# Norm weight, bias and alpha of the residual, moved from GpSimd to VectorE and from the norm to the next products

## The chip, the cores and the metric

One core of one Trainium2 chip. The metric is the device time of one execution in microseconds, as the median over runs. All data starts and ends in the chip's memory; float32 in and out.

## What is computed

Two layers of a diffusion block on 512 tokens of x and 256 of a context, 1024 channels wide. Each layer has a feed-forward (2816 wide, gated), four mixers side by side (windowed attention, a state space model, full attention, neighbourhood attention) with a common output product, and a second feed-forward. After each of the three branches comes a norm, post_norm; the norm's result is what the next branch reads, and times ALPHA it is also what the next branch's result is added to.

```python
ALPHA = (2 * DEPTH) ** 0.25          # DEPTH = 2

def post_norm(x, f, g, b):
    return layer_norm(ALPHA * x + f, g, b)

for l in range(DEPTH):
    x = post_norm(x, 0.5 * m[:, 2] * swiglu(modulate(x, m[:, 0], m[:, 1]), ffn1_w_in[l], ffn1_w_out[l]), ln_g[l, 0], ln_b[l, 0])
    ...
    x = post_norm(x, m[:, 5] * mix_x, ln_g[l, 1], ln_b[l, 1])
    x = post_norm(x, 0.5 * m[:, 8] * swiglu(modulate(x, m[:, 6], m[:, 7]), ffn2_w_in[l], ffn2_w_out[l]), ln_g[l, 2], ln_b[l, 2])
```

The context goes through the same steps with its own modulations m; in the last layer only its first feed-forward and norm are needed.

## The kernel before, in words

**Tiles.** The residual lies in SBUF as six tiles res of 128 tokens by 1024 channels: XT are the four of x, CT the two of the context. Products run on TensorE in float32r, each operand split in two parts whose sum it is, so a product is three matmuls (mm3, L329 to L331). Weights come by DMA on SP's queue into wraw or wrax; ScalarE rounds them into the first part wh (L322), VectorE subtracts for the second part wl (L323). Six slots of wh and wl let the splits run ahead of the products.

**Stages in time.** First feed-forward of layer 0 to about 600 us, mixers to 1046, the merge (the mixers' output product) to 1110, second feed-forward to 1705; in layer 1 the feed-forward to 2255, mixers to 2620, merge to 2665, the last feed-forward to the end.

**A branch's end.** Each accumulated product of 512 columns is multiplied by its modulation (add, L468) and added to the residual (L470) on VectorE. stats (L411 to L436) takes mean and variance, finds the reciprocal root for two tiles at a time by a chain of 13 small VectorE instructions (rsqrt, L394 to L400, then L432), and ScalarE normalises the tiles in place (L436). Then turn transposes a normalised tile on TensorE (L383); ScalarE scales and shifts it by channel, with the norm's weight and bias folded in, into S (L385); the cast L387 and VectorE's subtraction L388 make the two parts acth and actl, the left operands of the next products. The four x tiles are turned first, the context's two later.

**The residual's addend.** The tile itself still holds the normalised values, without weight and bias. rescale makes of them what the next branch's result is added to: ALPHA * (g * x + b). Its gain (L447) loads weight and bias onto all partitions by two DMAs, ScalarE multiplies both by ALPHA (L456), and for each tile and each half of its columns GpSimd multiplies and adds in place (L461): four instructions of 128x512 for a tile, 112 in all. They must wait until TensorE has transposed the tile. rescale is a generator with one step for each tile. The x tiles' steps are taken at once after the norm (branch_out, ffn); the context's follow one for each chunk of the next feed-forward (winograd), or at the spill.

**The feed-forward.** Its 22 chunks of 128 columns of gate and up weights: the first two as plain products, the rest by Winograd's seven products, for which GpSimd makes sums of weight tiles (L605, L606, L611, L613) and VectorE sums of products (L688 to L702). The result is split into gTh and gTl (L642, L643). The chunks come in parts; after the chunks of a part (lo .. hi) their part of the second product is added to the residual.

**Mixers.** Their scratch takes the room of the residual, so spill_res copies it to DRAM (away, L362) and fetch_res brings it back (L366) before the merge.

**Order.** A scheduler of the tile framework sets each engine's order of instructions from the order in which the code records them and from hints (issue_after: not ahead of that instruction).

Of the kernel before, what the change touches and what calls it, by code (L numbers as in the profile page):

```python
# [20 lines left out]
D = 1024  # L21
# [5 lines left out]
CT = (4, 5)  # L27
# [7 lines left out]
# columns of mix_w_in after the host's reordering (heads of aq and cq as 0, 2, 1, 3)  # L35
C_A, C_Z, C_XBC, C_C, C_D, C_BDT = 0, 512, 768, 1536, 2048, 2816

# columns of the constants
# [4 lines left out]
BY_SUM = (0, 4, 1, 5, 2, 6, 3, 7)  # channel chunks in the order of the feed-forward's sums  # L43
K_ID, K_SEL = K_N, K_N + P
GATES = (2, 5, 8)  # the modulations that multiply a branch
N_SLOTS = 2 * len(GATES)
K_ALL = K_SEL + 4 * N_SLOTS
# columns of the neighbourhood masks
# [4 lines left out]
def _constants():  # L53
# [19 lines left out]
    # sums of the four groups' rows of the modulations; for those that multiply a branch, half of it  # L73
    # where it is a feed-forward's, with the bias in rows 16 and on
# [17 lines left out]
def bcast(ap, n):  # L92
    """Repeats the elements of a [p, a, ...] operand n times along a new last dimension."""
    s = list(ap.shape)
    return ap.unsqueeze(len(s)).to_broadcast(s + [n])


def bcast1(ap, n):
    """Repeats a [p, ...] operand n times along a new first free dimension."""
    s = list(ap.shape)  # L100
    return ap.unsqueeze(1).to_broadcast([s[0], n] + s[1:])
# [12 lines left out]
def side_by_side(a, na, b, nb):  # L114
    """Runs two generators, of na and nb steps, so that both last as long."""
    i = j = 0
    while i < na or j < nb:
        if j >= nb or (i < na and i * nb <= j * na):
            next(a, None)
            i += 1  # L120
        else:
            next(b, None)
            j += 1
    for g in (a, b):
        for _ in g:
            raise AssertionError("more steps than told")


class Block:
    def __init__(self, ctx, tc, t, out):  # L130
# [7 lines left out]
        # the products' left operands, by channel, in two parts: inputs of the feed-forward and of  # L138
        # the mixers, then what the mixers give
# [25 lines left out]
    # ---------------------------------------------------------------- small parameters  # L165
    def turned(self, rows, tag):
        """Vectors cut in rows of 128, turned so that the channel is the partition."""
# [16 lines left out]
    def conditioning(self):  # L184
        """silu(c) and silu(c_ctx) as stationary operands: any two of 32 columns, the others zero."""
# [13 lines left out]
        # modulations by channel: layer, which of the nine, chunk, stream  # L199
# [39 lines left out]
    def ada_batch(self, l, ns, pool, at_once=()):  # L239
        """Two steps for each of these 512 columns of both streams' modulations; the last also places them: by  # L240
        channel (a shift and a scale's, in order), or, of what multiplies a branch, as rows in DRAM."""
# [48 lines left out]
    def mod_affine(self, l, i, halves=((0, KD),), into=None):  # L290
        """Scale and shift, by channel, of what follows norm i of layer l (i = -1: the input)."""
# [15 lines left out]
    # ---------------------------------------------------------------- weights and products  # L307
    def weights(self, src, shape):
        """Loads float32 weights, contraction chunks by columns, and splits each chunk into two float32r parts
        whose sum it is."""  # L310
# [6 lines left out]
    def split_slot(self, raw, slot=None):  # L317
        """The two parts of chunks [p, chunk, columns], in up to 512 columns."""
# [7 lines left out]
    def mm3(self, out, a, b, start, stop):  # L326
        """out += a'b with a and b given in two parts."""
# [8 lines left out]
    # ---------------------------------------------------------------- residual stream  # L336
# [14 lines left out]
    def scale_input(self):  # L351
# [4 lines left out]
    def spill_res(self, n):  # L356
        """The residual's addend waits in DRAM while the mixers run."""
        for _ in self.behind:
            pass
# [8 lines left out]
    def new_sums(self, pool, tiles):  # L368
        """Room for what the feed-forward's sums come from: act's value, by channel chunk."""
# [3 lines left out]
    def turn(self, tiles, aff, ks=range(KD)):  # L373
        """xT of these token tiles: turned, scaled and shifted by channel, split."""
# [15 lines left out]
    def rsqrt(self, tmp, x, n, mul=1.0):  # L390
        """(x * mul + EPS) ** -0.5 of n columns: a guess from the exponent, three Newton steps."""
# [11 lines left out]
    def stats(self, t, dh, tmp, gain=None):  # L403
        """Mean and variance of the token tile's half; after a pair's last, the pair normalised in place; with
        gain, each tile by itself, and the result of it put out."""
# [37 lines left out]
    def gain(self, l, i, tmp, tags):  # L443
        """A norm's gain and bias, on all partitions."""
# [5 lines left out]
    def rescale(self, l, i, tiles, tmp):  # L450
        """Normalised tiles times the gain and plus the bias, times alpha: the next residual's addend. One step
        for each tile."""
        nc = self.nc
        gb = self.gain(l, i, self.side or tmp, ("mrow0", "mrow1"))
        for x in gb:
            nc.scalar.mul(x, x, ALPHA)  # L456
        for t in tiles:
            for lo, hi in ((0, 512), (512, D)):
                for x, op in zip(gb, (ALU.mult, ALU.add)):
                    r = self.res[t][:, lo:hi]  # L460
                    nc.gpsimd.tensor_tensor(r, r, x[:, lo:hi], op=op)  # L461
            yield

    def add(self, t, dh, acc, mrow, tmp, norm, gain=None):
        """512 columns of a product, times its modulation, to the residual."""
# [8 lines left out]
    def branch_out(self, l, i, tiles, steps, a_of, w_of, mrow, tmp, todo=None):  # L474
        """Adds a product, times its modulation, to the residual, 512 columns at a time; with todo, what
        comes of normalised tiles by number, the normalisation and that.

        steps: weight tiles' contraction chunks, in order; w_of(step, dh) loads one; a_of(k, t) the left
        operand's parts."""
# [29 lines left out]
        if norm:  # L509
            self.behind = self.rescale(l, i, tiles, tmp)  # L510
            for _ in XT if len(tiles) == 6 else XT[:3]:
                next(self.behind)

    def follow(self, todo, upto, end):
        """After products of which end is the last: what follows token tiles up to this one."""
# [4 lines left out]
    def turns(self, aff, tmp, tiles):  # L520
        """What to do when a token tile is normalised."""
# [5 lines left out]
    def mod_rows(self, l, which, pool, streams):  # L527
        """The modulation that multiplies a branch, on all partitions."""
# [7 lines left out]
    # ---------------------------------------------------------------- feed-forward  # L536
    # The first product, of all tokens A and a chunk's gate and up weights B: with tokens and channels
    # halved, A21 the second tokens' first channels, and B12 the up weights' first channels, Winograd's seven
    # products:
    #   S1 = A21 + A22, S3 = A11 - A21, S2 = A22 - S3, S4 = A12 - S2  # L540
    #   T1 = B12 - B11, T3 = B22 - B12, T2 = T3 + B11, T4 = B21 - T2
    #   U = A11 B11 + S2 T2, C11 = A11 B11 + A12 B21, C12 = U + S4 B22 + S1 T1,
    #   C21 = U + S3 T3 + A22 T4, C22 = U + S3 T3 + S1 T1
    # The first chunks have the plain eight, while the sums come.
    def left(self, name):
        """Four channel chunks of half of the tokens, in two parts."""
# [6 lines left out]
    def sums(self, pool):  # L553
        """S2, S3 and S4, then S1 in A21's place: two steps of two channel chunks each, then one."""
# [32 lines left out]
    def ffn_weights(self, l, w_in, f, pool):  # L587
        """B11, B21, B22 and T1 .. T4 in two parts."""
# [24 lines left out]
        last = tt(y[:, 1], y[:, 1], x[:, 0], op=ALU.subtract)  # L613
        put("T1", y[:, 1])
        return w, last

    def ffn(self, l, w_in, w_out, which, i, with_ctx, pool, after, parts, extra=None, final=False, early=()):
        """extra: work for the gaps, by feed-forward chunk. after: called when the next modulation is due,
# [85 lines left out]
        for lo, hi in parts:  # L704
# [10 lines left out]
            if lo == 0:  # L715
                for _ in self.behind:
                    pass
# [830 lines left out]
```

## Time and profile before

| | |
|---|---|
| median of 3 runs | 3099.47 us (3094.49 to 3105.36) |
| profiled execution, span | 3101.0 us, 44820 instructions |
| TensorE (PE) busy | 2913.0 us, 94% |
| VectorE (DVE) busy | 2216.5 us, 71% |
| ScalarE (ACT) busy | 1172.8 us, 38% |
| GpSimd (POOL) busy | 734.8 us, 24%, of which L461 171.8 us |

The runs were timed without the profiler; the profile is of one more execution, for which the span alone is known, from its first to its last instruction. It lies inside the interval of the runs.

### The profile page before, as it was taken

What the parts mean: (1) busy time and instruction counts of PE and PEld (TensorE: products, weight loads), DVE (VectorE), ACT (ScalarE), POOL (GpSimd) and SP (SyncE); (2) the same over time, 40 slices, a digit from 0 to 9 for tenths busy, and PEclk for the clock granted to TensorE, in tenths of its full rate; (3) what the DMA queues carried; (4) which work ended last, traced back from release to release, by engine and by line L of the source; (5) the groups of instructions that cost most, each with busy time, mean ns of one, the idle gap of its engine ahead of it and who ended that gap; (6) DMA issues with size and microseconds to landing.
All of it is one profiled execution on the core that took longest, in us unless ns stands there. A gap on an engine that the chain in (4) does not pass through costs nothing.

```text
span 3101.0 us, 44820 instructions
## 1 busy us (share of the span) xinstructions
PE 2913.0 (94%) x16772; PEld 2485.0 (80%) x16772; DVE 2216.5 (71%) x4258; ACT 1172.8 (38%) x2153; POOL 734.8 (24%) x532
## 2 busy tenths in 40 slices
PE   8999999999999989999999799999989989889996
PEld 5888888778787767888888689998967777778886
DVE  5666667875757587666577976668786666888779
ACT  4333223342256443322233433332343356434333
POOL 1222212220112034221121531222150120234323
PEclk9999999999999999999999899999989999999998
DMA  6443334131133213544443122221222232233231
GB/s 207 156 143 125 111 105 136 60 106 41 42 85 61 89 55 89 177 133 132 129 156 118 60 68 68 68 82 49 68 93 67 70 80 64 75 115 88 82 96 69
DMA packets 319533, 296.17 MB, mean 96 GB/s; under 512 B 16631, under 2 KB 245071, under 8 KB 319059
## 3 DMA queue, kind: packets, MB, share of 16 engines
q1 hardware_dynamic: 318259, 290.80, 30.5%
q0 software_dynamic: 1056, 2.49, 0.4%
q8 instruction: 133, 2.18, 0.3%
q14 instruction: 85, 0.70, 0.1%
HBM read 270.52 MB, written 7.39 MB: 90 GB/s over the span
## 4 chain that ended last, share of the span: by engine, by line
PE 57%; DVE 17%; issue 3%; ACT 2%; DMA 1%; POOL 0%; DVEq 0%; SPq 0%; ACTq 0%; POOLq 0%
PE ps L329 8%; PE ps L331 8%; PE ps L330 8%; PE psp L329 7%; PE psp L330 7%; PE psp L331 7%; DVE wl L323 4%; PE ps L1025 2%; PE ps L1066 2%; PE psp L1082 2%; DVE actl L388 2%; DVE tmp L468 1%; PE ps L260 1%; DVE res L470 1%; ACT wh L322 1%
## 5 line engine op out<-in xcount | busy, mean ns | idle before, releaser
L323 DVE TENSOR_TENSOR wl<-wraw,wh 128x512 fp32r<-128x512 f32 x600 | 465.0, 782 | 341.7 <-ACT wh L322 336.2
L322 ACT CAST wh<-wraw 128x512 fp32r<-128x512 f32 x600 | 369.6, 620 | 897.3 <-PE ps L331 470.7
L329 PE MATMUL psp<-acth,wh 128*128 128x384 f32 (+2 forms) x1592 | 532.6, 335 | 24.1 <-DVE e L700 19.0
L330 PE MATMUL psp<-actl,wh 128*128 128x384 f32 (+2 forms) x1592 | 526.1, 331 | 2.7 <-DVE actl L388 2.7
L331 PE MATMUL psp<-acth,wl 128*128 128x384 f32 (+2 forms) x1592 | 524.6, 330 | 0.7 <-DVE wl L323 0.7
L329 PEld LDWEIGHTS psp<-acth,wh 128*128 128x128 f32 x1592 | 303.7, 191 | 72.9 <-ACT wh L322 49.0
L329 PE MATMUL ps<-S,wh 128*128 128x384 f32 (+1 forms) x960 | 315.2, 328 | 17.9 <-DVE ffg L638 7.7
L330 PEld LDWEIGHTS psp<-actl,wh 128*128 128x128 f32 x1592 | 303.5, 191 | 16.3 <-DVE actl L388 3.6
L331 PEld LDWEIGHTS psp<-acth,wl 128*128 128x128 f32 x1592 | 303.8, 191 | 12.8 <-issue 1.9
L331 PE MATMUL ps<-S,wl 128*128 128x384 f32 (+1 forms) x960 | 312.0, 325 | 1.2 <-DVE wl L323 1.2
L330 PE MATMUL ps<-S,wh 128*128 128x384 f32 (+1 forms) x960 | 312.0, 325 | 0.0
L461 POOL TENSOR_TENSOR res<-res,mrow 128x512 f32<-128x512 f32 x112 | 171.8, 1565 | 461.6 <-PE ps L383 340.8
L322 ACT CAST wh<-wrax 128x512 fp32r<-128x512 f32 x280 | 173.4, 620 | 271.6 <-PE ps L330 160.8
L323 DVE TENSOR_TENSOR wl<-wrax,wh 128x512 fp32r<-128x512 f32 x280 | 255.2, 918 | 7.2 <-ACT wh L322 6.2
L329 PE MATMUL ps<-wh,gTh 128*128 128x512 f32 x594 | 234.6, 395 | 8.3 <-DVE tmp L468 8.3
L331 PE MATMUL ps<-wh,gTl 128*128 128x512 f32 x594 | 233.4, 393 | 0.0
L330 PE MATMUL ps<-wl,gTh 128*128 128x512 f32 x594 | 233.1, 392 | 0.0
L330 PE MATMUL ps<-actl,wh 128*128 128x384 f32 (+2 forms) x568 | 202.5, 357 | 24.3 <-DVE actl L388 24.2
L329 PEld LDWEIGHTS ps<-S,wh 128*128 128x128 f32 x960 | 183.5, 191 | 42.8 <-ACT wh L322 26.7
L331 PE MATMUL ps<-acth,wl 128*128 128x384 f32 (+2 forms) x568 | 200.3, 353 | 8.1 <-DVE wl L323 8.1
L329 PE MATMUL ps<-acth,wh 128*128 128x384 f32 (+2 forms) x568 | 202.6, 358 | 3.7 <-ACT wh L322 2.3
L470 DVE TENSOR_TENSOR res<-res,tmp 128x512 f32<-128x512 f32 x268 | 190.9, 744 | 0.6
(369 smaller groups left out, 5727.4 us busy)
## 6 DMA issues: line engine op xcount, KB each, us to landing
araw<-in_ada_w_dram SPq DMA_DIRECT2D x128, 512.0 KB
wraw<-in_ffn_w_out_dram SPq DMA_DIRECT2D x88, 512.0 KB
wraw<-in_ffn_w_in_dram SPq DMA_DIRECT2D x160, 256.0 KB
wrax<-in_ffn_w_in_dram SPq DMA_DIRECT2D x160, 256.0 KB
wraw<-in_mix_w_in_dram SPq DMA_DIRECT2D x44, 512.0 KB
wraw<-in_ffn_w_in_dram SPq DMA_DIRECT2D x16, 512.0 KB
wraw<-in_mix_w_out_dram SPq DMA_DIRECT2D x16, 512.0 KB
mrow<-mrow SPq DMA_DIRECT2D x10, 512.0 KB
```

Source lines behind the costliest of these rows:

```text
L260: nc.tensor.matmul(ps[32 * g:32 * g + 32, :], lhsT=self.cs[:, k, c0:c0 + 32], rhs=w[:, k - kk, :], start=i == 0 and k < 4, stop=i == len(n ...
L322: self.nc.scalar.copy(h, raw)
L323: self.nc.vector.tensor_tensor(lo, raw, h.bitcast(F32), op=ALU.subtract)
L329: mm(out, lhsT=a[0], rhs=b[0], start=start, stop=False)
L330: mm(out, lhsT=a[0], rhs=b[1], start=False, stop=False)
L331: return mm(out, lhsT=a[1], rhs=b[0], start=False, stop=stop)
L388: nc.vector.tensor_tensor(l, y, h.bitcast(F32), op=ALU.subtract)
L461: nc.gpsimd.tensor_tensor(r, r, x[:, lo:hi], op=op)
L470: nc.vector.tensor_tensor(r, r, y, op=ALU.add)
L1025: nc.tensor.matmul(ps[:, at:at + hi - lo], lhsT=q, rhs=part[:, lo:hi], start=i == 0, stop=i == 1)
L1066: nc.tensor.transpose(pt[:, j * P:(j + 1) * P], p[:, a:a + P], self.ident)
L1082: nc.tensor.matmul(out[64 * a:64 * a + 64, :], lhsT=v[:, kt, vcol:vcol + 64], rhs=pT[:, i], start=i == 0, stop=i == len(order) - 1)
```

## The change

rescale runs its tensor_tensor instructions on VectorE and by halves: the first 512 columns of all tiles, then the second. Nothing of it is done at the norm any more: self.behind holds the call itself, and it is made where the next products come to be added. In a feed-forward that is after the chunks of the first part, in the merge at its start (after the residual is fetched, so that what is spilled is now the normalised tile). At the merge it takes only the tiles that the merge needs. winograd no longer takes a step of it, spill_res no longer drains it. scale_input (the scaling of the kernel's input, on VectorE before and after) takes two arguments that it does not use, to be called in the same way. A side pool for gains is closed one chunk later (ada 4 for 3). The comments, which are removed too, are left out here.

```diff
-    def rescale(self, l, i, tiles, tmp):
+    def rescale(self, l, i, tmp, tiles=XT + CT, tags=("mrow0", "mrow1")):
         nc = self.nc
-        gb = self.gain(l, i, self.side or tmp, ("mrow0", "mrow1"))
+        gb = self.gain(l, i, self.side or tmp, tags)
         for x in gb:
             nc.scalar.mul(x, x, ALPHA)
-        for t in tiles:
-            for lo, hi in ((0, 512), (512, D)):
+        for lo, hi in ((0, 512), (512, D)):
+            for t in tiles:
                 for x, op in zip(gb, (ALU.mult, ALU.add)):
                     r = self.res[t][:, lo:hi]
-                    nc.gpsimd.tensor_tensor(r, r, x[:, lo:hi], op=op)
+                    nc.vector.tensor_tensor(r, r, x[:, lo:hi], op=op)
             yield
...
     def spill_res(self, n):
-        for _ in self.behind:
-            pass
...
         if norm:
-            self.behind = self.rescale(l, i, tiles, tmp)
-            for _ in XT if len(tiles) == 6 else XT[:3]:
-                next(self.behind)
+            self.behind = partial(self.rescale, l, i)
...
         def winograd(f, g, rest):
-            w, last = self.ffn_weights(l, w_in, f, pool)
-            if with_ctx or f > 3:  # of fewer tokens, after the sums
-                with self.tc.issue_after(last.ins):
-                    next(self.behind, None)
+            w = self.ffn_weights(l, w_in, f, pool)
...
             if lo == 0:
-                for _ in self.behind:
+                for _ in self.behind(pool, tiles):
                     pass
...
             if not final:
-                self.behind = self.rescale(l, i, tiles, pool)
-                for _ in XT:
-                    next(self.behind)
+                self.behind = partial(self.rescale, l, i)
...
     def merge(self, l, last, tmp):
         tiles = XT if last else XT + CT
+        for _ in self.behind(tmp, tiles, ("mrow1", "mrow2") if last else ("mrow0", "mrow1")):
+            pass
...
-        ada = {3: [aside]}
+        ada = {4: [aside]}
```

The lines of the changed kernel have other numbers: its L459 is L461 of before, L466 and L468 are L468 and L470, L392 to L398 are the root's L394 to L400, L430 is L432, L385 and L386 are L387 and L388, L360 is L362.

In the order of the instructions, VectorE before the first addition of layer 0's merge, as it was (res are the residual's tiles, wl second parts of weights, actl those of the merge's left operand):

```order
L1137 SCALAR_TENSOR_TENSOR actl_65<-ps_1983_9866,smT_378,acth_64 128x256
L323 TENSOR_TENSOR wl_10061<-wraw_10054,wh_10060 128x512
L323 TENSOR_TENSOR wl_10137<-wraw_10134,wh_10136 128x512
L323 TENSOR_TENSOR wl_10141<-wraw_10134,wh_10140 128x512
L323 TENSOR_TENSOR wl_10183<-wraw_10180,wh_10182 128x512
L323 TENSOR_TENSOR wl_10187<-wraw_10180,wh_10186 128x512
L323 TENSOR_TENSOR wl_10193<-wraw_10190,wh_10192 128x512
L468 TENSOR_TENSOR tmp_10100<-psp_9912,mrow_1993_9894 128x512
```

And as it is in the changed kernel; of the 24 L459 the last ones are shown, the 21 others stand right ahead of them, behind wl_10061:

```order
L459 TENSOR_TENSOR res_1986_9849<-res_1986_9849,mrow_1992_9865 128x512
L459 TENSOR_TENSOR res_1987_9850<-res_1987_9850,mrow_1992_9865 128x512
L459 TENSOR_TENSOR res_1988_9851<-res_1988_9851,mrow_1991_9864 128x512
L323 TENSOR_TENSOR wl_10137<-wraw_10134,wh_10136 128x512
L459 TENSOR_TENSOR res_1988_9851<-res_1988_9851,mrow_1992_9865 128x512
L323 TENSOR_TENSOR wl_10141<-wraw_10134,wh_10140 128x512
L323 TENSOR_TENSOR wl_10183<-wraw_10180,wh_10182 128x512
L323 TENSOR_TENSOR wl_10187<-wraw_10180,wh_10186 128x512
L466 TENSOR_TENSOR tmp_10100<-psp_9912,mrow_1993_9894 128x512
```

The weight differences that followed one another now stand behind the block of L459, and wl_10193 behind the first additions.

The second place is VectorE after the merge of layer 0, at the context's reciprocal root (rs), before:

```order
L398 TENSOR_TENSOR rs_2092_10455<-rs_2091_10454 128x2
L399 SCALAR_TENSOR_TENSOR rs_2092_10455<-rs_2092_10455,rs_2090_10453 128x2
L400 SCALAR_TENSOR_TENSOR rs_2091_10454<-rs_2092_10455,rs_2091_10454 128x2
L432 SCALAR_TENSOR_TENSOR bnm_10468<-bnmv_10364,rs_2091_10454 128x2
L387 CAST acth_64<-S_1997_9904 128x256
```

The same place in the changed kernel, the last round of the root and what follows it:

```order
L396 TENSOR_TENSOR rs_2092_10455<-rs_2091_10454 128x2
L459 TENSOR_TENSOR res_1985_9848<-res_1985_9848,mrow_2203_11133 128x512
L397 SCALAR_TENSOR_TENSOR rs_2092_10455<-rs_2092_10455,rs_2090_10453 128x2
L459 TENSOR_TENSOR res_1986_9849<-res_1986_9849,mrow_2203_11133 128x512
L398 SCALAR_TENSOR_TENSOR rs_2091_10454<-rs_2092_10455,rs_2091_10454 128x2
L459 TENSOR_TENSOR res_1983_9846<-res_1983_9846,mrow_2202_11132 128x512
L430 SCALAR_TENSOR_TENSOR bnm_10468<-bnmv_10364,rs_2091_10454 128x2
L459 TENSOR_TENSOR res_1984_9847<-res_1984_9847,mrow_2202_11132 128x512
L634 TENSOR_TENSOR ffg_10628<-ps_2104_10522,ffg_10628 128x512
```

One L459 stands between every two steps of the root; behind its last step more of them stand ahead of the context's first cast. The remaining ones stand among the first Winograd chunks.

The third place is SP's queue at the start of layer 0's mixers (wraw here the mixers' weight tiles), before:

```order
L313 DMA wraw_5501<-in_mix_w_in_dram 128x8x128
L447 DMA mrow_987_5363<-in_ln_g_dram 128x1024
L313 DMA wraw_5571<-in_mix_w_in_dram 128x8x128
L313 DMA wraw_5644<-in_mix_w_in_dram 128x8x128
L447 DMA mrow_988_5364<-in_ln_b_dram 128x1024
L313 DMA wraw_5715<-in_mix_w_in_dram 128x8x128
L362 DMA away_5393<-res_4_78 128x1024
L362 DMA away_5393<-res_5_79 128x1024
```

In the changed kernel:

```order
L313 DMA wraw_5400<-in_mix_w_in_dram 128x8x128
L313 DMA wraw_5471<-in_mix_w_in_dram 128x8x128
L360 DMA away_5363<-res_4_78 128x1024
L360 DMA away_5363<-res_5_79 128x1024
L360 DMA away_5363<-res_6_80 128x1024
L360 DMA away_5363<-res_7_81 128x1024
L313 DMA wraw_5541<-in_mix_w_in_dram 128x8x128
```

The x tiles' spills moved from behind the fifth weight tile to behind the second, and the loads of the norm's weight and bias left this place.

## Rows read from the trace of the kernel before

**Rows 1.** The page: busy shares, chain by engine.

```profile
PE 2913.0 (94%) x16772; PEld 2485.0 (80%) x16772; DVE 2216.5 (71%) x4258; ACT 1172.8 (38%) x2153; POOL 734.8 (24%) x532
...
PE 57%; DVE 17%; issue 3%; ACT 2%; DMA 1%; POOL 0%; DVEq 0%; SPq 0%; ACTq 0%; POOLq 0%
```

**Rows 2.** The line L461: count, ns (min/median/max), first and last start.

```profile
L461 POOL TENSOR_TENSOR res<-res,mrow x112: 1253/1646/1892, 599.9 to 2747.8; 128x512 f32<-128x512 f32 x112
```

**Rows 3.** Busy time by stretch: us, PE, PEld, DVE, ACT, POOL, PEclk, DMA, GB/s.

```profile
599.90:627.70 27.80, 18.19 (x61) 12.21 (x59) 27.41 (x30) 7.99 (x13) 23.88 (x16) 0.82 0.35 120
1111.90:1138.70 26.80, 15.06 (x59) 10.35 (x57) 26.44 (x29) 6.89 (x13) 25.35 (x16) 0.85 0.18 58
1706.90:1733.50 26.60, 13.89 (x60) 8.87 (x58) 26.36 (x26) 6.97 (x12) 25.37 (x16) 0.89 0.20 61
2255.80:2283.60 27.80, 18.01 (x61) 12.21 (x59) 27.42 (x30) 8.00 (x13) 23.49 (x16) 0.82 0.34 120
2672.00:2684.20 12.20, 6.38 (x35) 5.55 (x33) 11.96 (x15) 1.86 (x5) 11.68 (x8) 0.86 0.29 86
```

**Rows 4.** Chain of the stretch 1109 to 1140 us: start, duration, what.

```profile
1110.83 0.33 DVE acth L387
1111.17 0.60 DVE res L470
1111.77 0.60 DVE actl L388
1112.37 1.43 DVE acth L387
...
1133.70 1.15 DVE rs L398
...
1137.32 0.17 DVE rs L398
```

**Rows 5.** VectorE's groups by form, 1111.9 to 1138.7 us: count, busy us, mean ns.

```profile
L388 DVE TENSOR_TENSOR actl<-S,acth 128x512 fp32r<-128x512 f32 x8 | 12.7, 1611 | 0.0
...
L323 DVE TENSOR_TENSOR wl<-wraw,wh 128x512 fp32r<-128x512 f32 x3 | 2.0, 679 | 0.0
```

**Rows 6.** TensorE's waits, 599.5 to 650 us: total us, times, longest.

```profile
PE ps L330 <- DVE actl L388: 8.7, 6, 2.2
```

**Rows 7.** TensorE's waits, 1111 to 1160 us.

```profile
PE ps L383 <- ACT res L436: 5.9, 1, 5.9
PE ps L331 <- DVE wl L323: 5.3, 1, 5.3
```

**Rows 8.** Busy time by stretch, behind the first of rows 3.

```profile
627.70:650.00 22.30, 18.81 (x113) 16.39 (x114) 15.89 (x23) 12.87 (x24) 11.94 (x8) 0.92 0.18 64
```

**Rows 9.** VectorE's groups by form over the run.

```profile
L323 DVE TENSOR_TENSOR wl<-wrax,wh 128x512 fp32r<-128x512 f32 x280 | 255.2, 918 | 7.2 <-ACT wh L322 6.2
L470 DVE TENSOR_TENSOR res<-res,tmp 128x512 f32<-128x512 f32 x268 | 190.9, 744 | 0.6
```

**Rows 10.** Busy time by stretch, ahead of the merges' first additions.

```profile
1046.00:1074.00 28.00, 27.78 (x128) 22.82 (x129) 9.37 (x19) 7.83 (x12) 0.00 (x0) 1.00 0.57 216
2628.00:2643.00 15.00, 15.00 (x67) 12.41 (x67) 5.52 (x9) 4.35 (x7) 0.00 (x0) 1.00 0.54 175
```

**Rows 11.** VectorE's groups by form over the run: the context's casts.

```profile
L387 DVE CAST acth<-S 128x256 fp32r<-128x256 f32 x28 | 12.8, 461 | 18.4 <-ACT S L385 18.3
```

**Rows 12.** Busy time by stretch, first Winograd chunks.

```profile
1170.00:1200.00 30.00, 24.28 (x129) 23.04 (x128) 28.75 (x34) 12.69 (x24) 19.37 (x13) 0.94 0.43 130
2700.00:2770.00 70.00, 59.62 (x437) 57.60 (x438) 64.22 (x103) 32.87 (x68) 30.17 (x21) 0.92 0.37 113
```

**Rows 13.** VectorE's groups by form, 1172.9 to 1196 us.

```profile
L323 DVE TENSOR_TENSOR wl<-wrax,wh 128x512 fp32r<-128x512 f32 x7 | 10.1, 1456 | 0.0
L323 DVE TENSOR_TENSOR wl<-wraw,wh 128x512 fp32r<-128x512 f32 x3 | 4.2, 1397 | 0.0
```

**Rows 14.** GpSimd's groups by form, 2693 to 2750 us.

```profile
L606 POOL TENSOR_TENSOR wraw<-wraw 128x512 f32<-128x512 f32 x2 | 2.8, 1408 | 9.8 <-DVE wl L323 9.8
```

More of the change, by code (lines that the diff above doesn't have):

```diff
@@ L349, in load_streams, with scale_input @@
             self.nc.sync.dma_start(self.res[i], src)
-    def scale_input(self):
+    def scale_input(self, pool, tiles):
         for r in self.res:
@@ L612, in ffn_weights @@
         put("T4", y[:, 0])
-        last = tt(y[:, 1], y[:, 1], x[:, 0], op=ALU.subtract)
+        tt(y[:, 1], y[:, 1], x[:, 0], op=ALU.subtract)
         put("T1", y[:, 1])
-        return w, last
+        return w
     def ffn(self, l, w_in, w_out, which, i, with_ctx, pool, after, parts, extra=None, final=False, early=()):
@@ L1461, in layers @@
         b.constants()
-        b.behind = b.scale_input()
+        b.behind = b.scale_input
         ada = {}
```

## The prediction

> **What bounds the kernel now.** Start with the page's busy shares and chain. TensorE is busy for 94% of the span and carries 57% of the chain that ended last; VectorE carries 17% of it, GpSimd nothing [rows 1]. By shares alone, moving 112 GpSimd instructions of about 1.6 us [rows 2] to VectorE only loads an engine that matters. But a share is a mean, so the next view is the stretches. In the five stretches in which GpSimd runs its first L461 instructions after a norm (the fifth is shorter, 12 us), VectorE is busy for the whole stretch while TensorE is busy for 14 to 18 of 27 us, at a granted clock of 0.82 to 0.89 [rows 3]. In these 121.2 us TensorE is busy for 18.19 + 15.06 + 13.89 + 18.01 + 6.38 = 71.5 us and idle for 49.7.
>
> Why is VectorE so slow there? In the chain after the merge of layer 0 the same instruction changes its duration the moment L461 begins (1111.9 us): the cast L387 takes 0.33 us at 1110.83 and 1.43 at 1112.37, the subtraction L388 takes 0.60 at 1111.77, the two-column steps of the reciprocal root take 1.15 us and, once L461 is over at 1137.3, 0.17 [rows 4]. The mean of L388 in the stretch is 1611 ns; weight differences between the root's steps keep their 679 [rows 5]. So what GpSimd does off the chain is paid on the chain: two thirds of VectorE's time in these stretches is contention. TensorE waits there for VectorE's two parts (8.7 us, L388) or for the normalised context tile (5.9 us, L436) and a weight difference (5.3 us, L323) [rows 6, 7].
>
> **What the change removes.** All 112 instructions leave GpSimd; 104 come to VectorE, because layer 1's first norm now scales only the four x tiles at the merge (8 fewer). The two ScalarE multiplications per norm and the DMAs of gain and bias only change place.
>
> One stretch priced again without contention, the second of rows 3 (29 instructions, 26.44 us): eight L388 at 0.60, three L387 at 0.33, three weight differences and one L411 at 0.6, thirteen steps of the root's chain at 0.17 + 0.02 between them: 4.8 + 1.0 + 2.4 + 2.5 = 10.7 us. It saves 15.7 us of chain. The first stretch has 30 such instructions and comes to 11.5: 15.9 saved; the third is taken as the second, the fourth as the first. The fifth (15 instructions, eleven of the root and four splits) comes to about 4.2 us: 7.8 saved.
>
> How much of a chain saving reaches the end? TensorE's own work in the stretch must still be done, so a floor is its idle time there, and the idle of the 22 us behind it, where the second GpSimd run falls (22.3 - 18.8 = 3.5 in the first case) [rows 8]. For the norms ahead of the mixers: idle 9.6 + 3.5 = 13.1, chain 15.9, and some waiting for casts remains, because 0.60 + 0.33/2 per channel chunk is still no faster than TensorE's products of it. I take **12 each, 24** (9 to 16).
>
> **What it adds, place by place.** A VectorE instruction of the moved form (two SBUF inputs, 128x512) is there already: L470 at 744 ns mean [rows 9], 0.60 us to the next one in the chain [rows 4]. So 104 x 0.60 = 62 us come to VectorE; what counts is where.
>
> *Merge of layer 0* (24 instructions, nearly all in one piece ahead of the first addition). From 1046 to 1074 VectorE is busy 7.83 of 28 us, TensorE 27.78 [rows 10]. 24 x 0.60 = 14.4 us fit in the 20 idle ones; a weight difference behind the burst comes late, but the splits run several chunks ahead. Cost 0; if the cover fails, two of the 0.69 us differences and the 4 us between them, 4.
>
> *Merge of layer 1* (16, 9.6 us). From 2628 to 2643 VectorE has 15 - 4.35 = 10.6 us idle [rows 10], so it just fits, but two weight differences that stood ahead of the first addition now stand behind it. I take 2 (0 to 5).
>
> *The norms ahead of the second feed-forward of layer 0 and the first of layer 1.* Eight of 15 or 16 stand between the steps of the context's root, whose last step releases ScalarE and then TensorE: 8 x 0.60 = 4.8 us on the chain. The other seven or eight stand ahead of the first cast of the context, which before waited 18.3 us in four norms for ScalarE, 4.6 each [rows 11]: 4.2 to 4.8 us, covered. So 15.7 - 4.8 = **11 each, 22**. TensorE's idle there, 11.7 and 12.7 us, agrees. The remaining eight or nine go into the first two Winograd chunks. VectorE is busy for 28.75 of 30 us there [rows 12], so each counts: 9 x 0.60 = 5.4, or 9 x 0.92 = 8.3 beside GpSimd's sums, the price of a weight difference from the other buffer [rows 9]. Removed in the same place: seven such differences at 1456 ns and three at 1397 while L461 ran [rows 13], against 0.68 [rows 5]: 5.4 + 2.2 = 7.6. Net 0 (-2 to +1 each).
>
> *The last feed-forward* (16). Three stand in the norm (1.8 us), thirteen in the chunks up to the first products' additions, where VectorE is busy for 64.22 of 70 us [rows 12]. 13 x 0.60 to 0.92 = 8 to 12; some 5 of contention goes, and 5.8 us of idle takes a part: 3 left (0 to 7). With the 7.8 saved and the merge's 2: **1**.
>
> *The spills ahead of the mixers.* On SP four copies of 0.5 MB now stand ahead of the third weight tile, not behind the fifth. At the 216 GB/s that the merge shows [rows 10] they take about 10 us, while two loaded tiles feed TensorE: 0 taken, 0 to 3 each.
>
> *Clock.* TensorE's 71.5 busy us in the five stretches ran at 0.82 to 0.89; at full clock they would be about 10 shorter. The clock stays partly down as long as some waiting remains: 3 taken.
>
> **Sum:** 24 + 22 + 1 + 3 = 50. The profiled execution has a span of 3101.0 us against the median of 3099.5: 0.05% apart, so I set the one against the other without correction. **3050 us.** About 9.3 us (0.3%) is what a measurement here can tell from no change.
>
> **The rivals.**
>
> *Smaller gain.* The places that I cost at nothing cost: Winograd chunks at 8.3 without the whole of the 7.6 returned (2 x 5), the last feed-forward 7 instead of 3, merges 4 and 5 instead of 0 and 2, spills 3 each: 10 + 4 + 7 + 6 = 27, so -23: 3077 us. For it: VectorE is full in just these chunks [rows 12]. Against it: the merge's idle [rows 10].
>
> *Larger gain.* Every stretch gives its whole chain saving and the clock: 15.9 x 2 + 10.9 x 2 + 7.8 + 10 + the context runs' 8 = 79: 3020 us.
>
> *No change.* The contention moves along with the work: each of the 9 + 8 + 13 = 30 instructions that come into Winograd chunks waits out one of the GpSimd sums left there, 1.4 us [rows 14]. 30 x 1.4 = 42, which takes the gain: 3092, or 3099 with a little more given back. Against it: weight differences beside the same sums average 0.92 against 0.68 us [rows 9], so about one in six waits a whole sum.
>
> The Trainium skill has a rule for it in "SBUF — State Buffer", section Who interferes with whom: a VectorE instruction with two SBUF inputs contends with a GpSimd instruction that reads SBUF, and whoever issues first holds the shared ports for its whole instruction. By that rule the moved instructions, which have two SBUF inputs, would keep meeting GpSimd in the chunks, and the sum would tend to this rival's 3092. The trace agrees as to the kind [rows 4] but not as to every instruction [rows 5, 9].
>
> *Slower: VectorE becomes the bound.* Of the removed contention only TensorE's direct waits return, some 13 in each of four norms, and these are partly needed for ScalarE's normalisation: say 30. The new 62 us lie on a full VectorE (71% busy over the run [rows 1]) and at 0.92 in the Winograd chunks: 62 + 30 x 0.32 = 72 on the path. That is +42, 3141; with the merge's 14 hidden +28, 3128. It decides where the merges and norms have under half of the idle time that I count. Against it: 26 us of VectorE's chain per norm are mostly contention, which goes whatever is added.
>
> By the Trainium skill's "Perfetto Trace Analysis", section Optimizing Scalar/DVE Operations, work is offloaded from a saturated VectorE to other engines, GpSimd among them, the reverse of this change; the same section doubts it between these two. By the first half of that sentence the slower rival holds; the two durations of one cast [rows 4] bear out the doubt.
>
> *It does not do what it says.* The instruction order shows L459 on VectorE and none on GpSimd, so this is left at nothing.
>
> **Chances.** Forecast 0.55, smaller gain 0.24, larger 0.10, no change 0.05, slower 0.06. Faster by over 0.3%: 0.55 + 0.24 + 0.10 - 0.01 for the weak end = 0.88; within: 0.06; slower: 0.06. The range, 3020 to 3083, goes from the larger gain to just past the smaller one; left out are no change, slower and the tails.
>
> **What would show it.** Right: L388 at about 0.6 and the root's steps at 0.17 after each norm; the five stretches 10 to 15 us shorter; L432 releasing ScalarE sooner; VectorE's L459 at 0.6 to 0.7 in the merges with no new wait of TensorE at the first addition, and 0.9 or more in the Winograd chunks. Wrong: TensorE waiting in the merges for the weight differences, in the mixers' first projections for loads, or Winograd chunks longer by 5 us or more each.

## The result and the profile after

The changed kernel takes 3021.96 us (median of 4 runs, 3019.45 to 3025.41) against 3098.93 for the kernel before in the same comparison: 77 us less, ratio 0.975 with a 95% interval of 0.9735 to 0.9765. The forecast was 3050 in a range of 3020 to 3083: the time lies inside, at its fast end, where the "larger gain" stood.

The page of the changed kernel, the lines that answer to [rows 1] and [rows 2] (busy shares, chain by engine, and the costliest form of the weight differences):

```profile
PE 2880.9 (95%) x16772; PEld 2461.7 (82%) x16772; DVE 2161.1 (72%) x4362; ACT 1174.5 (39%) x2153; POOL 570.0 (19%) x420
...
PE 75%; DVE 17%; issue 3%; ACT 2%; DMA 2%; POOL 0%; SPq 0%; DVEq 0%; ACTq 0%; POOLq 0%
...
L323 DVE TENSOR_TENSOR wl<-wrax,wh 128x512 fp32r<-128x512 f32 x280 | 241.4, 868 | 9.9 <-ACT wh L322 9.0
```

The first thing to read is VectorE. It has 104 instructions more, which at 0.68 us are 71 us, and yet it is busy for 55 us less: 2161 against 2216. So its other work became about 126 us shorter without a line of it being changed. The second is the chain, and it has to be read with care. TensorE's share is 75%, against 57% [rows 1], but both are shares of the span, and the chain of before could be followed back only to 640 us: its shares add up to 80%. From the same matmul on (number 3161, at 640 us before and 620 after) TensorE carries 71% of the chain before and 73% after, VectorE 21% and 18%. The third is TensorE's own busy time, which fell by 32 us (2913.0 to 2880.9) with the same 16772 matmuls.

The scaling at its new engine: L459, count, ns (min/median/max), first and last start.

```profile
L459 DVE TENSOR_TENSOR res<-res,mrow x104: 672/680/1779, 1031.7 to 2682.7; 128x512 f32<-128x512 f32 x104
```

On GpSimd its median was 1646 ns. In the stretches after the norms, the counterparts of [rows 3] (us, then busy us of PE, PEld, DVE, ACT, POOL, then PEclk, DMA share, GB/s):

```profile
600.60:620.00 19.40, 19.11 (x107) 15.02 (x106) 14.37 (x41) 14.57 (x26) 0.00 (x0) 1.00 0.64 196
1089.00:1116.00 27.00, 24.23 (x127) 19.45 (x127) 26.93 (x60) 18.53 (x32) 5.65 (x4) 1.00 0.23 72
1656.50:1682.00 25.50, 25.05 (x124) 20.23 (x124) 24.24 (x59) 15.73 (x22) 0.00 (x0) 1.00 0.28 84
2197.00:2216.00 19.00, 18.79 (x97) 14.79 (x96) 18.72 (x48) 13.36 (x20) 0.00 (x0) 1.00 0.36 110
```

TensorE is busy for 98% of three of them and 90% of the second, at a granted clock of 1.00 where it was 0.82 to 0.89. The counterpart of the fifth stretch still has 0.83:

```profile
2602.00:2612.00 10.00, 9.37 (x65) 8.73 (x65) 6.18 (x23) 9.02 (x18) 0.00 (x0) 0.83 0.25 80
```

VectorE's forms after the merge of layer 0 (1085 to 1112 us), which answer to [rows 5]: L386 is L388 of before.

```profile
L459 DVE TENSOR_TENSOR res<-res,mrow 128x512 f32<-128x512 f32 x15 | 9.8, 677 | 0.0
L386 DVE TENSOR_TENSOR actl<-S,acth 128x512 fp32r<-128x512 f32 x8 | 5.2, 678 | 0.1
...
L385 DVE CAST acth<-S 128x512 fp32r<-128x512 f32 x4 | 1.7, 415 | 0.0
```

L386 is at 678 ns, from 1611. Its chain there shows the new interleaving, and that it is cheap:

```profile
1098.67 0.59 DVE wl L323
1099.26 0.07 DVE rs L396
1099.33 0.60 DVE res L459
1099.93 0.07 DVE rs L397
1100.00 0.60 DVE res L459
...
1105.31 0.07 DVE bnm L430
1105.38 0.60 DVE res L459
1105.99 0.60 DVE ffg L634
1106.59 3.01 DVE res L459 x5
1109.60 0.41 DVE acth L385 x2
```

A step of the root with one scaling instruction takes 0.67 us; alone under L461 it took 1.15 [rows 4]. The first cast of the context starts 4.2 us after the root's last step; before the change it was 4.6 us ([rows 11] has the 18.3 us of four norms). So the instructions that were put there are hidden, as the prediction said.

**Where the 77 us came from.** Both kernels issue 16772 matmuls, so the same matmul can be looked up by its number in both traces (some 570 stand up to 48 places away). The table is worked out in that way: a stretch between two matmuls, its length before and after in us, and how much of the difference is idle time between matmuls and how much is time in which TensorE was busy.

| stretch | before | after | difference | idle | busy |
|---|---|---|---|---|---|
| first norm and start of the mixers, layer 0 | 81.1 | 60.7 | -20.4 | -12.8 | -7.6 |
| merge, layer 0 | 73.5 | 73.3 | -0.2 | 0.0 | -0.2 |
| its norm, to the third Winograd chunk or so | 164.8 | 154.0 | -10.8 | -9.1 | -1.7 |
| second feed-forward's norm, layer 0, same | 98.9 | 84.1 | -14.8 | -11.6 | -3.2 |
| first norm and start of the mixers, layer 1 | 159.5 | 138.5 | -21.0 | -11.3 | -9.7 |
| merge, layer 1 (matmuls 14125 to 14325) | 43.1 | 46.1 | +3.0 | +1.8 | +1.3 |
| its norm and the last feed-forward's first chunks | 176.3 | 161.2 | -15.2 | -6.2 | -9.0 |

Together 79 of the 83.3 us by which the two spans differ (3101.0 and 3017.7; the medians differ by 77, and single runs of one kernel by up to 11). 49 us are idle time, 30 us the same matmuls done faster, and that is the granted clock: what it lacked during TensorE's busy time adds up to 59.0 us over the run before and 25.7 after. The merges took 40 of the 104 instructions. The first lost nothing by it; the second became 3 us longer, and TensorE's waits there (2555 to 2600 us) are part of that:

```profile
PE psp L329 <- DVE tmp L466: 1.2, 2, 0.6
PE ps L329 <- DVE tmp L466: 0.4, 1, 0.4
```

### The profile page after: what moved, and what is told of

Same layout as the page of the kernel before. It is cut to its first block, busy times and chain, and to the rows that moved or that the text cites. A ratio compares the mean times of both kernels' runs of the same rounds, so it can differ in the third digit from the quotient of the medians.

```text
span 3017.7 us, 44777 instructions
## 1 busy us (share of the span) xinstructions
PE 2880.9 (95%) x16772; PEld 2461.7 (82%) x16772; DVE 2161.1 (72%) x4362; ACT 1174.5 (39%) x2153; POOL 570.0 (19%) x420
## 4 chain that ended last, share of the span: by engine, by line
PE 75%; DVE 17%; issue 3%; ACT 2%; DMA 2%; POOL 0%; SPq 0%; DVEq 0%; ACTq 0%; POOLq 0%
PE ps L329 11%; PE ps L331 11%; PE ps L330 11%; PE psp L329 10%; PE psp L331 9%; PE psp L330 9%; DVE wl L323 3%; PE ps L260 2%; PE ps L1016 2%; PE ps L1057 2%; PE psp L1073 2%; DVE tmp L466 2%; DVE res L468 1%; DVE res L459 1%; DVE actl L386 1%
## 5 line engine op out<-in xcount | busy, mean ns | idle before, releaser
L329 PE MATMUL psp<-acth,wh 128*128 128x384 f32 (+2 forms) x1592 | 529.7, 333 | 28.1 <-DVE e L693 23.6
L323 DVE TENSOR_TENSOR wl<-wrax,wh 128x512 fp32r<-128x512 f32 x280 | 241.4, 868 | 9.9 <-ACT wh L322 9.0
L329 PE MATMUL ps<-acth,wh 128*128 128x384 f32 (+2 forms) x568 | 195.4, 346 | 2.8 <-ACT wh L322 1.7
L330 PE MATMUL ps<-actl,wh 128*128 128x384 f32 (+2 forms) x568 | 193.4, 341 | 0.1
L331 PE MATMUL ps<-acth,wl 128*128 128x384 f32 (+2 forms) x568 | 192.6, 339 | 0.0
L468 DVE TENSOR_TENSOR res<-res,tmp 128x512 f32<-128x512 f32 x268 | 188.0, 732 | 0.6
L331 PEld LDWEIGHTS ps<-S,wl 128*128 128x128 f32 x960 | 182.0, 190 | 1.6 <-issue 0.9
```

What stands on the lines that cost most here:

```text
L323: self.nc.vector.tensor_tensor(lo, raw, h.bitcast(F32), op=ALU.subtract)
L329: mm(out, lhsT=a[0], rhs=b[0], start=start, stop=False)
L330: mm(out, lhsT=a[0], rhs=b[1], start=False, stop=False)
L331: return mm(out, lhsT=a[1], rhs=b[0], start=False, stop=stop)
L468: nc.vector.tensor_tensor(r, r, y, op=ALU.add)
```

## The experiments

Two theories stood against each other. The one of the prediction: GpSimd's work, wherever its result is needed, slows VectorE, VectorE makes TensorE wait. The other: the change also moves the scaling to a later place, and it may be this that wins. The clock was a third question: its part of the gain was ten times what had been forecast.

### The engine alone

```diff
-                    nc.gpsimd.tensor_tensor(r, r, x[:, lo:hi], op=op)
+                    nc.vector.tensor_tensor(r, r, x[:, lo:hi], op=op)
```

in the kernel before.

> The kernel before with one word changed: the scaling at L461 runs on VectorE, at the norm as before. Theory (what GpSimd did beside VectorE was the loss, wherever the scaling stands): the 1.2 to 1.7 us durations after the norms vanish here too, and about 16 instructions of 0.6 us stand in or right behind the context's root chain, as they do in the changed kernel ahead of two of the feed-forwards, where 16 and 18 us were won. So about 12 to 15 us less at each of four norms and 5 to 10 at the fifth: 3030 to 3050 us. Rival (it is the later place that wins, not the engine): within 10 us of 3099.

Measured: 3029.41 us, ratio 0.9772 (0.9758 to 0.9787). Of the 77 us, 71 come from the engine, a little more than the theory had; TensorE's busy time is again part of it (2884.8 us, 28 less than before). The rival falls. What the later place adds is small, and the two intervals touch. By the matmul numbers the early place costs 5 us at each norm ahead of a mixer (24.1 us against 18.7 for the first hundred matmuls after it) and 7 and 4 us at the norms ahead of the feed-forwards with a context (38.2 against 31.1, 46.9 against 42.6). It wins some of it back in the Winograd chunks after the merge (37.0 against 40.8 for the matmuls 6300 to 6500, 78.0 against 82.1 for the four hundred behind them).

### The place alone

```diff
-                    nc.vector.tensor_tensor(r, r, x[:, lo:hi], op=op)
+                    nc.gpsimd.tensor_tensor(r, r, x[:, lo:hi], op=op)
```

in the changed kernel.

> The changed kernel with one word put back: the scaling runs on GpSimd, at its new place. Theory: in the merges 24 and 16 instructions of 1.3 to 1.6 us (about 34 and 23 us) don't end before the first addition, so TensorE waits there some 10 to 15 us in the first and 5 to 10 in the second; ahead of the feed-forwards GpSimd is free and takes them at the norm again, so three norms stay slow. Won are the two norms ahead of the mixers, 20 us each, less the merges' waits: 3075 to 3095 us. Rival (the later place wins): about 3022, as the changed kernel.

Measured: 3094.49 us, ratio 0.9981 (0.9972 to 0.999), at the upper end of what was expected. The two norms ahead of the mixers are as quick as in the changed kernel (18.7 us for the first hundred matmuls, as there). The other three stay slow, as expected: a hundred matmuls there take 44.3, 38.1 and 24.3 us, against 36.5, 39.0 and 25.9 before and 21.6, 20.7 and 14.3 in the changed kernel. The merges pay too, 15 and 12 us. The waits in the first, TensorE's and ScalarE's (to 1090 and 1100 us), name another mechanism than the one expected:

```profile
PE psp L329 <- ACT wh L322: 12.7, 1, 12.7
...
ACT mrow L454 <- DMA mrow<-in_ln_g_dram: 20.5, 1, 20.5
```

TensorE waits not at the first addition but for a rounded weight. ScalarE stands still for 20.5 us at L454, the multiplication of the next norm's gain by ALPHA, which is ahead of that weight in its order; the gain's load comes late. That it comes late because GpSimd still reads the gain before it, in the same buffer, is argued, not shown. So the place without the engine is worth almost nothing.

### GpSimd at work for nothing

```diff
+    def for_nothing(self, tmp, count):
+        n = self.half
+        y, e = self.y[KD - 1][:, :n], self.sb(tmp, [n], "e0")
+        self.nc.gpsimd.tensor_tensor(e, y, y, op=ALU.subtract)
+        for _ in range(count):
+            self.nc.gpsimd.tensor_tensor(e, e, e, op=ALU.mult)
...
             self.behind = partial(self.rescale, l, i)
+            self.for_nothing(tmp, 20 if len(tiles) == 6 else 15)
...
                 self.behind = partial(self.rescale, l, i)
+                self.for_nothing(pool, 20)
```

> The changed kernel, and after each of the five norms, once the x tiles are transposed, 21 GpSimd instructions of 128x384 (16 of 128x256 at the fifth) on a scratch tile, which nothing waits for. The result is the same. Theory (GpSimd's reading of SBUF slows VectorE): the first runs of the kernel before are back, VectorE's casts and root steps take 1.2 to 1.7 us again, the granted clock falls to 0.8 to 0.9: 10 + 15 + 18 + 11 + 11 us come back, 3075 to 3095 us. Rival (waits for the scaling's result or for its buffers were the loss): nothing waits for this work, so 3022 within 10.

Measured: 3076.72 us, ratio 0.9918 (0.9897 to 0.9938): 55 us of the 77 are back, by work on which nothing depends. VectorE's forms at the first norm (595 to 640 us) show how:

```profile
L386 DVE TENSOR_TENSOR actl<-S,acth 128x512 fp32r<-128x512 f32 x8 | 6.4, 836 | 0.0
L386 DVE TENSOR_TENSOR actl<-S,acth 128x256 fp32r<-128x256 f32 x8 | 6.4, 833 | 0.1
L385 DVE CAST acth<-S 128x256 fp32r<-128x256 f32 x4 | 2.8, 706 | 4.6 <-ACT S L383 4.6
```

The same forms in the changed kernel, in the same stretch:

```profile
L386 DVE TENSOR_TENSOR actl<-S,acth 128x512 fp32r<-128x512 f32 x8 | 5.1, 677 | 0.0
L386 DVE TENSOR_TENSOR actl<-S,acth 128x256 fp32r<-128x256 f32 x8 | 3.2, 423 | 1.2 <-ACT acth L385 1.0
L385 DVE CAST acth<-S 128x256 fp32r<-128x256 f32 x4 | 1.2, 290 | 3.5 <-ACT S L383 3.5
```

The half-wide subtractions, 423 ns undisturbed, take 833; the granted clock of the stretch from 600 to 640 us is 0.91. The useless instructions were shorter than L461 (means of 1046 and 1565 ns), and the second runs of L461, for the context's tiles, were not copied; by the matmul numbers the stretch of the first norm is still 9 us quicker than before (72.1 us against 81.1). Contention is shown as a cause by itself.

### GpSimd that only writes

```diff
-            self.nc.gpsimd.tensor_tensor(e, e, e, op=ALU.mult)
+            self.nc.gpsimd.memset(e, 0.0)
```

with twice the count, in the kernel of the last experiment.

> As the run with 21 idle GpSimd instructions after each norm, but 40 fills of the scratch tile (they read nothing) in their place after one that reads. Theory (it is GpSimd's reading that collides with VectorE's second input): 3022 within 10, root steps at 0.17 us. Rival (any work on GpSimd in that stretch slows VectorE): a loss of the same kind as with the reading instructions, in proportion to the fills' busy time.

Measured: 3030.23 us, ratio 0.9772 (0.9758 to 0.9787). GpSimd is busy for 17 us after the first norm, as with the reading instructions (18), and VectorE's subtractions do not notice; its casts do (595 to 640 us: three forms, and the fills):

```profile
L386 DVE TENSOR_TENSOR actl<-S,acth 128x512 fp32r<-128x512 f32 x8 | 5.1, 677 | 0.0
L386 DVE TENSOR_TENSOR actl<-S,acth 128x256 fp32r<-128x256 f32 x8 | 3.2, 425 | 0.6 <-ACT acth L385 0.4
L385 DVE CAST acth<-S 128x256 fp32r<-128x256 f32 x4 | 2.2, 548 | 3.5 <-ACT S L383 3.4
...
L516 POOL MEMSET e<- 128x384 f32 x40 | 16.9, 422 | 2.3
```

So it is not that GpSimd works. What counts for the subtractions, which have two inputs in SBUF, and for most of the kernel's time is that GpSimd reads; in what else a fill differs from a multiplication was not tested apart. A cast has one input, and the four half-wide casts, all beside fills, take 548 ns instead of 290, so writing alone is not free. The 8 us above the changed kernel are spread (1 us at the first norm, 2 us in the Winograd chunks after the merge, 1 to 3 us elsewhere) and just inside what was expected; whether the slower casts are behind them was not looked into.

The Trainium skill states this in "SBUF — State Buffer", section Who interferes with whom: a VectorE instruction with two SBUF inputs contends with a GpSimd instruction that reads SBUF, not with one that only writes it. The two runs agree, with 833 ns and 425 ns for the same subtraction.

### The moved work left out

```diff
-                for x, op in zip(gb, (ALU.mult, ALU.add)):
-                    r = self.res[t][:, lo:hi]
-                    nc.vector.tensor_tensor(r, r, x[:, lo:hi], op=op)
+                pass
```

> The changed kernel without the 104 scaling instructions (weight, bias and alpha are left off the residual; the loads of the gains stay). It tells what the moved work still costs on VectorE. Theory (most of it is hidden; on the path are some eight instructions in each of two root chains, those in full Winograd chunks, and the last merge's few): 3022 less 15 to 30, 2992 to 3007 us. Rival (VectorE is now the bound, each of the 104 x 0.68 = 71 us counts): 2950 to 2960.

This kernel leaves the scaling out, so it shows what the work costs and computes something else. Measured: 2998.5 us, ratio 0.9671 (0.9658 to 0.9684). The 71 us of VectorE's new work cost 23 us, a third. About half of it is paid behind the two norms ahead of feed-forwards with a context: from 40.8 to 36.4 us for the matmuls 6300 to 6500, behind the merge's norm, with 2 us more just ahead of them, and from 41.5 to 35.1 for 9300 to 9500, behind the next. The last feed-forward's first chunks have 3 us (58.4 to 55.4), the second merge 2 (46.1 to 43.9).

### The feed-forwards' scaling held back

```diff
-            nc.vector.tensor_tensor(gl, g, gh.bitcast(F32), op=ALU.subtract)
+            return nc.vector.tensor_tensor(gl, g, gh.bitcast(F32), op=ALU.subtract)
...
-                store(g, f, lo)
+                stored = store(g, f, lo)
             if lo == 0:
-                for _ in self.behind(pool, tiles):
-                    pass
+                with self.tc.issue_after(stored.ins):
+                    for _ in self.behind(pool, tiles):
+                        pass
```

> The changed kernel, with the feed-forwards' scaling held back behind the last chunk of the first part, so that it runs beside the second product, as one block ahead of the first addition. Theory: the 15 to 16 instructions leave the context's root chain and the first cast, the others leave the full Winograd chunks; beside the second product VectorE has room. 5 to 10 us less at each of the two inner feed-forwards, 0 to 5 at the last: 3000 to 3015 us. Rival (they were covered where they stood, or the block now delays the first addition): 3022 or more.

Measured: 3007.86 us, ratio 0.9703 (0.969 to 0.9716), 14 us less than the changed kernel: faster than both. The scheduler had taken the recorded place as the latest, not as the wanted one, and put the instructions ahead wherever VectorE had a gap, which is at the norm. Held back, the 24 of the second feed-forward run as one block, 1161 to 1175 us, beside the second product:

```profile
L459 DVE TENSOR_TENSOR res<-res,mrow x24: 684/692/699, 1161.2 to 1175.0; 128x512 f32<-128x512 f32 x24
```

The same two hundred matmuls behind the two norms now take 36.3 and 34.8 us, as without any scaling. TensorE waits 2.7 us at the first additions; some 4 us are given back in the rest of layer 1's first feed-forward (429.6 us against 425.7).

### VectorE at work for nothing

The function for_nothing as above, on nc.vector, with 44 instructions behind the first one (30 at the fifth norm).

> The changed kernel, and after each norm 45 VectorE instructions of 128x384 (31 of 128x256 at the fifth) on a scratch tile, in the root chain and behind it; GpSimd has nothing to do there. It makes TensorE wait as long as before the change without GpSimd. Theory (the granted clock falls because TensorE idles, whoever makes it idle): some 10 us of idle return at each norm, the clock falls under 0.95 in those stretches, and the time lost is clearly more than the idle that was added (1.3 to 1.7 times): 3070 to 3110 us. Rival (the clock fell with the work of GpSimd): the clock stays at 0.99 or 1 and only the idle counts.

Measured: 3088.18 us, ratio 0.9962 (0.9949 to 0.9976). TensorE's stretches of 25 us after the merge, first of this kernel, then of the changed one:

```profile
1110.00:1135.00 25.00, 22.03 (x146) 19.50 (x145) 21.77 (x53) 13.21 (x25) 14.09 (x4) 1.00 0.12 34
1135.00:1160.00 25.00, 9.92 (x52) 8.52 (x50) 24.80 (x40) 6.80 (x13) 11.98 (x6) 0.78 0.33 103
```

```profile
1110.00:1135.00 25.00, 20.65 (x136) 18.22 (x135) 25.00 (x47) 16.40 (x35) 7.11 (x6) 1.00 0.15 45
1135.00:1160.00 25.00, 21.22 (x112) 20.39 (x111) 23.18 (x32) 9.89 (x18) 11.69 (x7) 0.93 0.27 83
```

In the second stretch GpSimd does the same in both (11.98 and 11.69 us), and TensorE idles for 15 us instead of 4: the clock is 0.78 instead of 0.93. By the matmul numbers the 23.6 us that were lost there are 17.0 of idle time and 6.5 of slower matmuls; at the next norm 24.9 are 17.4 and 7.5: 1.4 times the idle, within what was expected. So the clock fell here with TensorE's idle time, and no more work of GpSimd was needed for it. At the first norm the same 45 instructions cost only 10 us, with 0.97 granted from 590 to 650 us: there TensorE had x's products to do meanwhile.

### By tiles instead of halves

```diff
-        for lo, hi in ((0, 512), (512, D)):
-            for t in tiles:
+        for t in tiles:
+            for lo, hi in ((0, 512), (512, D)):
```

> The changed kernel, with the scaling by tiles again, both halves of a tile before the next, as the kernel before had it. Theory: in the merges all of it stands ahead of the first addition in either order, so the halves bring nothing: 3022 within 6. Rival (the halves let the first additions start earlier): 5 to 15 us more, in the merges.

Measured: 3019.57 us, ratio 0.974 (0.9726 to 0.9753), the same as the changed kernel. The halves do nothing in this kernel.

## Why the prediction was right, and where it was not

The time lies in the range, 28 us below the forecast. The idle time was forecast well, and nearly all of the miss is one term, the clock. That the fast end of the range covers it is in part luck: that end was a sum with 10 us of clock and larger chain savings than came.

- *What bounds the kernel.* Right: VectorE's slow stretches under L461, not GpSimd's time. Shown from both sides: the engine changed alone gives 71 of 77 us, reading instructions that nothing needs take 55 back. "Two thirds" was a little high: by the prediction's own sums 15.7 of 26.4 us are contention. Its opening figures of the chain, 57% and 17%, are shares of a span that the chain covers only from 640 us on; no term rests on them.
- *The norms ahead of the mixers, 12 each.* As idle time right: 12.8 and 11.3. The spills ahead of the weights cost nothing in layer 0: all that TensorE waits for between 595 and 645 us is 0.2 us.
- *The norms ahead of feed-forwards, 11 each.* As idle time 9.1 and 11.6. The root's chain costs what was said (a 0.60 between two steps), and the context's first cast hides the rest. Of the Winograd chunks the prediction had a net of 0, -2 to +1 each; the matmul numbers have +4.7 in length for those after the merge (+1.8 for 6300 to 6500, +2.9 for 6500 to 6900) and +3.5 for the others (9300 to 9500); 1.7 and 2.3 us of that are idle time. Not all of it is the moved instructions: the kernel without scaling still takes 81.3 us for 6500 to 6900, against 79.1 before and 82.1 after. Why is open. L459 takes 816 ns there, between the two prices of 0.60 and 0.92:

```profile
L323 DVE TENSOR_TENSOR wl<-wraw,wh 128x512 fp32r<-128x512 f32 x9 | 8.5, 983 | 1.8 <-ACT wh L322 1.8
L459 DVE TENSOR_TENSOR res<-res,mrow 128x512 f32<-128x512 f32 x8 | 6.4, 816 | 0.0
L323 DVE TENSOR_TENSOR wl<-wrax,wh 128x512 fp32r<-128x512 f32 x7 | 5.9, 854 | 0.0
```

  (VectorE's forms, 1112 to 1160 us.) Holding the work back from these places, the first casts and the last feed-forward's chunks is worth the 14 us measured.
- *The merges, 0 and 2.* As idle time 0.0 and 1.8, so the costs were right. Their reason was misread: the columns of [rows 10] are PE, PEld, DVE, ACT, and 7.83 and 4.35 us are ScalarE's busy time. VectorE's is 9.37 and 5.52, which leaves it 18.6 us idle for the first 14.4 and 9.5 for the second 9.6. So the second does not fit, by a little, and it is the one that became longer. Without the scaling it takes 43.9 us instead of 46.1, which is the 2.
- *The last feed-forward, 1 with its merge.* Too low: 6.2 us of idle time went, 4.4 with the merge's 1.8 taken off. The norm (matmuls 14325 to 14500) gave 6.3, where 7.8 less 1.8 was forecast. The thirteen instructions in its chunks do cost 3 us (the run without them), but the contention that left the same chunks was worth as much, which the prediction had counted short.
- *Sum of the idle.* 24 + 22 + 1 = 47 forecast, 49 measured.
- *The clock, 3.* This is the step that was mis-sized: 30 us. It failed twice. The prediction took only the five stretches of [rows 3], where 71.5 busy us at full clock would be some 10 shorter, and left out what lies behind, though it had 0.92 in [rows 8] and 0.94 and 0.92 in [rows 12]. Behind the other four stretches the kernel before has less:

```profile
1138.70:1160.00 21.30, 20.02 (x122) 17.76 (x123) 16.64 (x34) 15.83 (x30) 4.51 (x4) 0.87 0.03 7
1733.50:1755.00 21.50, 19.38 (x112) 17.18 (x113) 16.76 (x37) 13.46 (x26) 4.60 (x4) 0.81 0.00 1
2283.60:2306.00 22.40, 20.19 (x116) 17.85 (x117) 16.21 (x23) 13.75 (x25) 13.28 (x9) 0.85 0.29 93
2684.20:2700.00 15.80, 9.99 (x55) 8.17 (x55) 11.67 (x17) 10.49 (x20) 8.52 (x8) 0.80 0.00 0
```

  Busy time times what the clock lacks, 20.02 x 0.13 and so on, makes another 11 us; [rows 8] adds 1.5 and the chunks of [rows 12] another 6. With the 10 that is some 29 us, so a size near the measured 30 stood in the trace before. And it took a third of its 10, "as long as some waiting remains"; the changed kernel has the full clock in the four long stretches, though TensorE is still idle for 2.8 us in one of them.
- *The rivals.* The "larger gain" came, at 79 forecast and 77 measured, though by another sum: its 10 us of clock were too few and its chain savings of 15.9 too many. VectorE did not become the bound; a third of its new work is on the path. The contention did not move along with the scaling: L459 waits some, 816 ns, not a whole sum of 1.4 us.

## What to carry to other kernels

An engine that is on no chain can still be the cause of one: compare the duration of the same instruction inside and outside the other engine's spans before pricing a move by busy shares. Where TensorE waits and the granted clock is low, price the idle time and the clock apart, and the clock also in the stretches behind the wait. The scheduler of this kernel's framework takes a late place in the code as a permission; where the gap it finds is in a critical chain, hold the work back explicitly.

## What was not expected

The clock's price: 17 us of idle time of TensorE, made by VectorE alone, cost another 6.5 to 7.5 us in slower matmuls, at a granted clock of 0.78 in the stretch that shows it. And that VectorE's weight differences kept their 679 ns in the middle of L461's run [rows 5] when they stood right behind a two-column step, while that step took 1.15 us instead of 0.17 [rows 4]: in these rows it is the small step that waits, and the long instruction behind it passes.
